# Norm statistics in a two-layer diffusion backbone: four channel chunks' matmuls issued side by side, squares of x kept in y

## The chip, the cores and the metric

One NeuronCore of a Trainium2 chip runs the whole forward pass. The metric is the time of one execution in microseconds of device time; of several runs the median is taken. Lower is better.

## What is computed

The reference is a backbone of two layers over 256 latent tokens and 256 context tokens, 1024 channels, all in float32. Every sub-layer (half feed-forward, mixer, half feed-forward) is wrapped in two RMS norms over the channels, one ahead of it and one behind it:

```
def rms_norm(x, gain):
    xf = x.astype(f32)
    xf = xf * lax.rsqrt(jnp.mean(jnp.square(xf), axis=-1, keepdims=True) + RMS_EPS)
    return (xf * gain.astype(f32)).astype(x.dtype)
def half_ffn(h, g_in, g_out, mod, w1, w3, w2):
    y = swiglu(pre_norm(h, g_in, mod), w1, w3, w2)
    return post_residual(h, y, g_out, mod, 0.5)
```

The mixer of layer 0 is a bidirectional S5 scan, that of layer 1 a differential attention. The change concerns only the mean of squares inside `rms_norm`.

## The kernel before, in words

Activations lie with channels on the 128 partitions: `x` and `y` are tiles [128, 2, 8, 256], that is two halves h (C = 0 the context, L = 1 the latents), eight channel chunks k, 256 tokens. The sum of squares over channels is therefore a sum over partitions and over k, and it is TensorE that forms it. `stat_add` (L213) does one chunk: ScalarE squares [128, 256] into a buffer `sq` (L216), and TensorE multiplies it by 32 columns of ones (L218) into 32 rows of a PSUM bank `st`, rows 32j with j = k mod 4, where chunks k and k + 4 add up. The buffers `sq` come from a pool of four (L53) that every user takes in the order of the program.

`stat_end` (L241) copies the bank (L245, VectorE), sums the four row groups by a small matmul (L248), takes the inverse root by Newton steps on two-element tiles (L225 to L234, VectorE), and spreads it over the partitions by another matmul (L255). There are 21 such statistics of eight chunks: 168 calls of `stat_add`.
- Ten stand behind a sub-layer. In the last pass of a feed-forward's second product (`ff2`, L487 and L488) output chunk d takes 12 or 18 matmuls of 256 columns (L372 to L374; float32 is split into a high and a low part, three products), VectorE adds them to y (L487), and `stat_add` follows for this d. The pass is done for half C, then for half L. The gate of S5 (`glu`, L1016) and the attention's output product (L1267) do the same.
- Eleven stand ahead of a sub-layer (`pre_stat`, L304): eight chunks of x, just after `post` (L277) has updated them on VectorE (L301). `pre` (L310) then writes y = x * scale * bc (L326) and its split into `hb` (L332, L333), on which the next products wait.

At a boundary of two sub-layers the program has this order: last pass for C, then post and pre for C, then last pass for L, then post and pre for L; the next sub-layer's first products begin with half C of its first three weight blocks. So C's norms run beside L's pass, and L's norms beside the next sub-layer's first products for C. Some matmuls are held back by hand: `QA = (0, 1, 6, 7)` lets the first products' chunk k = 0 follow L248 of L's post, k = 1 its L255, k = 6 the L248 of L's pre, k = 7 its L255 (`after` adds an order between two instructions of one engine).

The order on each engine is otherwise worked out ahead of the run by a planner that simulates the program; earlier instructions of the program have priority. The engines then run their lists strictly in order. Weights come by DMA into `stg`, ScalarE copies them to a high part `wh` (L352), VectorE forms the low part `wl` (L354). In layer 0's S5 part y is held in another layout ("mixed"): the chunks are interleaved in runs of 32 tokens, so that y[:, k] is a view of 8 runs; `yv(h, mixed)` (L261) gives either view.

One other place writes 32-row groups of one bank: `mod_pe` (L150) issues eight matmuls of 256 columns directly one after the other, over the four row groups twice.

Of the kernel before, what the change touches and what calls it, by code (L numbers as in the profile page):

```python
# [8 lines left out]
F32 = mybir.dt.float32  # L9
F32R = mybir.dt.float32r  # L10
I32 = mybir.dt.int32
AF = mybir.ActivationFunctionType
# [6 lines left out]
H = 256  # L19
# [13 lines left out]
class Net:  # L33
# [174 lines left out]


    def stat_begin(self):  # L210
        return self.ps_st.tile([128, 2 * H], F32, name="st")

    def stat_add(self, part, k, src):  # L213
        nc = self.nc
        sq = self.sq_p.tile([128, H], F32, name="sq")
        nc.scalar.activation(out=sq if len(src.shape) == 2 else sq.rearrange("p (t c) -> p t c", t=8), in_=src, func=AF.Square)  # L216
        j = k % 4
        nc.tensor.matmul(part[32 * j:32 * j + 32, 0:H], self.ones[:, 0:32], sq, start=(k < 4), stop=(k >= 4))  # L218

    def newton(self, r, v, n):  # L220

# [79 lines left out]
                    nc.vector.scalar_tensor_tensor(out=xk, in0=y[:, k], scalar=self.mod[:, l, s, 2, k, h:h + 1], in1=xk,  # L301
                                                   op0=ALU.mult, op1=ALU.add)

    def pre_stat(self, h):  # L304
        part = self.stat_begin()
        for k in range(ND):
            self.stat_add(part, k, self.x[:, h, k])
        return self.stat_end(part)

    def pre(self, l, s, h, split=True, mixed=False, bc=None, pool=()):  # L310
        nc = self.nc
        if bc is None:
            bc = self.pre_stat(h)
        if pool:
            bp = self.spread(bc)
        y = self.yv(h, mixed)
        los = []
        for k in range(ND):
            scale, shift = (self.mod[:, l, s, i, k, h:h + 1] for i in (1, 0))
            if k in pool:  # L320
                yk, xk = y[:, k], self.x[:, h, k].rearrange("p (t c) -> p t c", t=8)
                nc.gpsimd.tensor_tensor(out=yk, in0=xk, in1=bp.rearrange("p (t c) -> p t c", t=8), op=ALU.mult)
                nc.gpsimd.tensor_scalar(out=yk, in0=yk, scalar1=scale, scalar2=shift, op0=ALU.mult, op1=ALU.add)
                continue
            with self.after(los[k - 2] if split and k >= 2 else None):
                nc.vector.scalar_tensor_tensor(out=y[:, k], in0=self.x[:, h, k].rearrange("p (t c) -> p t c", t=8),  # L326
                                               scalar=scale, in1=bc.rearrange("p (t c) -> p t c", t=8),
                                               op0=ALU.mult, op1=ALU.mult)
            if split:
                hi, lo = (self.hh(h, j)[:, k] for j in range(2))  # L330
                yk = self.y[:, h, k]
                nc.scalar.activation(out=hi, in_=yk, func=AF.Identity, bias=shift)  # L332
                los.append(nc.vector.scalar_tensor_tensor(out=lo, in0=yk, scalar=shift, in1=hi,  # L333
                                                          op0=ALU.add, op1=ALU.subtract))
            else:
                nc.scalar.activation(out=y[:, k], in_=y[:, k], func=AF.Identity, bias=shift)
# [941 lines left out]
def body(tc, a, out, stop=None):  # L1278
    with ExitStack() as es:
        n = Net(tc, a, es)  # L1280
        nc = tc.nc
        L, C = 1, 0

        def dump():
            nc.sync.dma_start(out[1], n.x[:, 1])
            nc.scalar.dma_start(out[0], n.x[:, 0])

        def mods(*spec):
            def job(l, s, k, d):
                return 2.3, lambda: n.mod_job(l, s, k, d, n.last.ins)  # L1290
            return [job(l, s, k, d) for l, lst in zip(spec[::2], spec[1::2]) for s, k in lst for d in range(ND)]

        def steps(g, n, w):
            return [(w, lambda: next(g, None)) for _ in range(n)]

        def mix(*lists):

            order = sorted(((i + 0.5) / len(l), k, i) for k, l in enumerate(lists) for i in range(len(l)))
            return [lists[k][i] for _, k, i in order]

        def jobs0(es):
            i, o = n.s5_in_maps(), n.s5_out_maps()
            m = n.mod_pe([(0, 2), (1, 0), (1, 1), (1, 2), (2, 0), (2, 1)])
            return [(0.0, lambda: n.s5_maps_pool(es))] + mix(steps(i, 33, 3.0), steps(o, 42, 3.0), steps(m, 49, 1.5))

        for h, part in n.ffn(0, 0, (C, L), jobs0):
            if h == C:
                n.mod_fin(0, 0, (2,))
                n.mod_fin(0, 1, (0, 1, 2))
                n.mod_fin(0, 2, (0, 1))  # L1310
            n.post(0, 0, h, part, pool=(5, 6, 7) if h == L else ())
            if stop == "00":
                continue
            n.pre(0, 1, h, split=False, mixed=True, pool=(5, 6, 7) if h == L else ())
            if h == C:
                p0 = tc.cur_priority
        if stop == "00":
            return dump()

        def dumpm():  # L1320
            for h in range(2):
                nc.vector.tensor_copy(n.x[:, h].rearrange("p k (t c) -> p k t c", t=8), n.yv(h, True))
            dump()

        if stop == "h0":
            return dumpm()
        for h, part in n.s5(p0):
            if stop == "ymix0":
                continue
            n.post(0, 1, h, part, mixed=True)  # L1330
            if stop == "01":
                continue
            n.pre(0, 2, h)
        if stop == "ymix0":
            return dumpm()
        if stop == "01":
            return dump()
        for h, part in n.ffn(0, 2, (C, L), lambda es: mods(0, [(2, 2)], 1, [(0, 0), (0, 1), (0, 2), (1, 0), (1, 1)])):
            if h == C:
                n.mod_fin(0, 2, (2,))  # L1340
                n.mod_fin(1, 0, (0, 1))
            n.post(0, 2, h, part)
            if stop != "02":
                n.pre(1, 0, h)
        if stop == "02":
            return dump()
        for h, part in n.ffn(1, 0, (C, L), lambda es: mods(1, [(1, 2), (2, 0), (2, 1), (2, 2)])):
            if h == C:
                n.mod_fin(1, 0, (2,))
                n.mod_fin(1, 1, (0, 1))  # L1350
            n.post(1, 0, h, part)
            if stop != "10":
                n.pre(1, 1, h)
        if stop == "10":
            return dump()
        n.mod_fin(1, 1, (2,), (L,))
        n.mod_fin(1, 2, (0, 1, 2), (L,))
        part = n.attn()
        if stop == "ymix1":
            n.x = n.y  # L1360
            nc.vector.memset(n.y[:, 0], 0.0)
            return dump()
        n.post(1, 1, L, part, half=(4, 6))
        if stop == "11":
            return dump()
        n.pre(1, 2, L)
        for h, part in n.ffn(1, 2, (L,)):
            n.post(1, 2, h, part, half=(4, 6))
        if stop == "12":
            return dump()  # L1370
        for i, e in ((0, 2), (2, 4), (4, 6), (6, 8)):
            nc.sync.dma_start(out[0][:, i:e], n.x[:, 1, i:e])
# [88 lines left out]
```

## Time and profile before

| what | value |
|---|---|
| median of 3 runs | 1941.02 us (1938.6 to 1942.37) |
| profiled execution, its own time | 1940.48 us |
| its span in the trace | 1938.7 us |
| TensorE busy | 1807.7 us, 93% of the span |
| VectorE, ScalarE, GpSimd busy | 65%, 37%, 8% |
| L218, the statistics' matmuls: busy | 76.4 us, 336 instructions |
| L216, the squares: busy | 33.1 us from x, 30.7 us from y |

The span is the traced part of the execution; 1.8 us of the execution's time lie around it. A float32 matmul shows as two MATMUL instructions, so 168 calls are 336 rows. Matmuls overlap in the trace (the next begins while the last drains), so what a matmul costs the stream is read from start to start and not from its duration.

### The profile page before, as it was taken

How to read it: one execution, taken by the hardware profiler on the slowest of the kernel's cores; microseconds unless marked ns; L12 is line 12 of the kernel's file. 1: busy time of each engine (PE TensorE's matmuls, PEld its weight loads, DVE VectorE, ACT ScalarE, POOL GpSimd, SP SyncE). 2: the span in 40 equal slices, each digit the busy share in tenths (PEclk: the TensorE clock that was granted, in tenths of full speed). 3: DMA queues.
4: the chain of work that ended last, by engine and by line, in shares of the span. 5: the costliest groups of instructions: out<-in, count | busy, mean ns of one | idle time of the engine just before them, and what ended most of it. 6: DMA issues, size and time to landing. Idle time of an engine off the chain costs nothing.

```text
span 1938.7 us, 29411 instructions
## 1 busy us (share of the span) xinstructions
PE 1807.7 (93%) x11600; PEld 1503.7 (78%) x11600; DVE 1253.0 (65%) x2914; ACT 715.0 (37%) x1286; POOL 149.3 (8%) x250
## 2 busy tenths in 40 slices
PE   7999999999747889999999999999998999779997
PEld 3877777777637768888888798888887988669996
DVE  5868877642797567977763675455437587655554
ACT  4542332321534544222222343222224455544442
POOL 0123423320211000000000000000000000000000
PEclk8999999999968999999999999999999999989998
DMA  8678878882277634655543144444322221125551
GB/s 319 189 256 267 255 246 248 255 276 101 84 250 242 225 131 153 227 183 186 174 164 109 66 142 166 149 162 154 127 78 74 87 88 66 38 96 184 183 176 64
DMA packets 74954, 321.94 MB, mean 166 GB/s; under 512 B 13984, under 2 KB 15392, under 8 KB 54336
## 3 DMA queue, kind: packets, MB, share of 16 engines
q1 hardware_dynamic: 55472, 273.61, 40.7%
q0 software_dynamic: 19200, 45.40, 8.1%
q8 instruction: 91, 1.49, 0.3%
q10 hardware_dynamic: 144, 1.05, 0.1%
q14 instruction: 47, 0.39, 0.1%
HBM read 296.53 MB, written 23.53 MB: 165 GB/s over the span
## 4 chain that ended last, share of the span: by engine, by line
PE 81%; DVE 8%; DMA 6%; ACT 3%; issue 2%; POOL 1%; DVEq 0%; SPq 0%; ACTq 0%; POOLq 0%
PE mm L372 15%; PE mm L373 15%; PE mm L374 15%; PE acc L372 8%; PE acc L373 7%; PE acc L374 7%; PE st L218 3%; DMA bs<-bw 2%; DMA pt<-pqt 1%; DVE wl L354 1%; DMA ws<-cs 1%; PE acc L130 1%; PE st L255 1%; PE st L150 1%; PE mm L911 1%
## 5 line engine op out<-in xcount | busy, mean ns | idle before, releaser
L372 PE MATMUL mm<-hb,wh 128*128 128x512 f32 (+1 forms) x1632 | 573.8, 353 | 7.0 <-ACT wh L352 2.7
L373 PE MATMUL mm<-hb,wl 128*128 128x512 f32 (+1 forms) x1632 | 567.8, 350 | 0.0
L374 PE MATMUL mm<-hb,wh 128*128 128x512 f32 (+1 forms) x1632 | 560.1, 349 | 0.0
L352 ACT ACTIVATE wh<-stg 128x1024 fp32r<-128x1024 f32 x312 | 330.9, 1067 | 549.6 <-PE acc L374 302.3
L354 DVE TENSOR_TENSOR wl<-stg,wh 128x1024 fp32r<-128x1024 f32 x312 | 380.4, 1223 | 187.3 <-ACT wh L352 186.0
L372 PEld LDWEIGHTS mm<-hb,wh 128*128 128x128 f32 x1632 | 311.6, 191 | 60.7 <-issue 14.2
L373 PEld LDWEIGHTS mm<-hb,wl 128*128 128x128 f32 x1632 | 311.3, 191 | 44.1 <-issue 3.7
L374 PEld LDWEIGHTS mm<-hb,wh 128*128 128x128 f32 x1632 | 306.5, 191 | 43.0 <-issue 3.9
L372 PE MATMUL acc<-gh,wh 128*128 128x256 f32 (+1 forms) x832 | 282.8, 340 | 6.3 <-DVE y L496 4.7
L373 PE MATMUL acc<-gh,wl 128*128 128x256 f32 (+1 forms) x832 | 278.3, 335 | 0.0
L374 PE MATMUL acc<-gl,wh 128*128 128x256 f32 (+1 forms) x832 | 277.8, 335 | 0.0
L372 PEld LDWEIGHTS acc<-gh,wh 128*128 128x128 f32 x832 | 156.7, 188 | 33.2 <-DVE y L496 6.4
L373 PEld LDWEIGHTS acc<-gh,wl 128*128 128x128 f32 x832 | 156.7, 188 | 21.8 <-issue 5.1
L192 DVE CUSTOM_DVE_ANT_0 wjk<-wad,sb 128x1024 bf16<-128x1024 f32 x136 | 166.1, 1221 | 9.8 <-DMA wad<-wadat 7.9
L374 PEld LDWEIGHTS acc<-gl,wh 128*128 128x128 f32 x832 | 156.2, 188 | 19.2 <-issue 1.6
L496 DVE TENSOR_TENSOR y<-y,acc 128x512 f32<-128x512 f32 (+1 forms) x112 | 68.0, 608 | 89.4 <-PE acc L374 89.0
L445 DVE TENSOR_TENSOR si<-si,mm 128x512 f32<-128x512 f32 (+1 forms) x85 | 52.3, 616 | 97.8 <-PE mm L374 97.6
L443 ACT ACTIVATE si<-mm 128x512 f32<-128x512 f32 (+1 forms) x85 | 46.0, 541 | 166.6 <-PE mm L374 166.3
L218 PE MATMUL st<-sq,cst 128*32 128x256 f32 x336 | 76.4, 419 | 18.5 <-ACT sq L216 11.5
L487 DVE TENSOR_TENSOR y<-y,acc 128x256 f32<-128x256 f32 x56 | 22.9, 418 | 71.3 <-PE acc L374 71.2
L1074 POOL DMA_DIRECT2D rope<-rope x1 | 0.6, 567 | 849.0 <-PE acc L374 849.0
L339 ACT ACTIVATE gh<-si 128x512 fp32r<-128x512 f32 (+1 forms) x88 | 49.8, 566 | 43.4 <-DVE si L445 43.3
(403 smaller groups left out, 2186.0 us busy)
## 6 DMA issues: line engine op xcount, KB each, us to landing
stg<-w SPq DMA_DIRECT2D x132, 1024.0 KB, 4.9
wad<-wadat SPq DMA_DIRECT2D x80, 512.0 KB, 3.7
wad<-wadq SPq DMA_DIRECT2D x48, 512.0 KB, 6.9
ws<-cs SPq DMA_DIRECT2D x27, 512.0 KB, 11.2
bt<-s5bt POOLq DMA_DIRECT2D x32, 256.0 KB, 5.8
pt<-pqt POOLq DMA_DIRECT2D x32, 256.0 KB, 7.4
cs<-cw POOLq DMA_DIRECT2D x32, 256.0 KB, 5.1
bs<-bw POOLq DMA_DIRECT2D x32, 256.0 KB, 6.8
```

The lines of the kernel that those rows point to most:

```text
L192: nc.vector.tensor_tensor_reduce(out=jk, in0=w, in1=self.sb[:, h, :], op0=ALU.mult, op1=ALU.add, scale=1.0, scalar=0.0, accum_out=self.mod ...
L218: nc.tensor.matmul(part[32 * j:32 * j + 32, 0:H], self.ones[:, 0:32], sq, start=(k < 4), stop=(k >= 4))
L339: self.nc.scalar.activation(out=hi, in_=src, func=AF.Copy)
L352: nc.scalar.activation(out=hi, in_=st[:, o:o + w], func=AF.Copy)
L354: e.tensor_tensor(out=lo, in0=st[:, o:o + w], in1=hi, op=ALU.subtract)
L372: nc.tensor.matmul(out, wh, xh, start=first, stop=False)
L373: nc.tensor.matmul(out, wl, xh, start=False, stop=False)
L374: self.pe_last = nc.tensor.matmul(out, wh, xl, start=False, stop=last)
L443: nc.scalar.activation(out=si, in_=z1, func=AF.Silu)
L445: nc.vector.tensor_tensor(out=gf, in0=si, in1=z3, op=ALU.mult)
L487: nc.vector.tensor_tensor(out=yd, in0=yd, in1=o, op=ALU.add)
L496: nc.vector.tensor_tensor(out=yd, in0=yd, in1=o, op=ALU.add)
```

## The change

`stat_add` only collects the square; with every fourth chunk it issues the four matmuls in the order 3, 0, 1, 2, each ordered behind the last by `after`. For x the squares go into y[:, k] (in the layout y was last used in, `was=True` behind S5), for y into the four `sq` buffers as before. Nothing is added to the DMA queues.

```diff
     def stat_begin(self):
+        self.sqs = []
         return self.ps_st.tile([128, 2 * H], F32, name="st")
-    def stat_add(self, part, k, src):
-        nc = self.nc
-        sq = self.sq_p.tile([128, H], F32, name="sq")
-        nc.scalar.activation(out=sq if len(src.shape) == 2 else sq.rearrange("p (t c) -> p t c", t=8), in_=src, func=AF.Square)
-        j = k % 4
-        nc.tensor.matmul(part[32 * j:32 * j + 32, 0:H], self.ones[:, 0:32], sq, start=(k < 4), stop=(k >= 4))
+    def stat_add(self, part, k, src, sq=None):
+        nc = self.nc
+        if sq is None:
+            sq = self.sq_p.tile([128, H], F32, name="sq")
+        o = sq if len(src.shape) == len(sq.shape) else sq.rearrange("p (t c) -> p t c", t=8)
+        nc.scalar.activation(out=o, in_=src, func=AF.Square)
+        self.sqs.append(sq)
+        if k % 4 == 3:
+            last = None
+            for j in (3, 0, 1, 2):
+                po = part[32 * j:32 * j + 32, 0:H]
+                if len(self.sqs[j].shape) == 3:
+                    po = po.rearrange("p (t c) -> p t c", t=8)
+                with self.after(last):
+                    last = nc.tensor.matmul(po, self.ones[:, 0:32], self.sqs[j], start=(k < 4), stop=(k >= 4))
+            self.sqs = []
...
-    def pre_stat(self, h):
+    def pre_stat(self, h, mixed=False):
         part = self.stat_begin()
+        y = self.yv(h, mixed)
         for k in range(ND):
-            self.stat_add(part, k, self.x[:, h, k])
+            self.stat_add(part, k, self.x[:, h, k].rearrange("p (t c) -> p t c", t=8), y[:, k])
         return self.stat_end(part)
-    def pre(self, l, s, h, split=True, mixed=False, bc=None, pool=()):
+    def pre(self, l, s, h, split=True, mixed=False, bc=None, pool=(), was=False):
         nc = self.nc
         if bc is None:
-            bc = self.pre_stat(h)
+            bc = self.pre_stat(h, was)
...
             n.post(0, 1, h, part, mixed=True)
...
-            n.pre(0, 2, h)
+            n.pre(0, 2, h, was=True)
```

## Rows read from the trace of the kernel before

**Rows 1.** The profile's page: TensorE's busy time, and the chain that ended last by line (share of the span).
```profile
PE 1807.7 (93%) x11600; PEld 1503.7 (78%) x11600; DVE 1253.0 (65%) x2914; ACT 715.0 (37%) x1286; POOL 149.3 (8%) x250
PE mm L372 15%; PE mm L373 15%; PE mm L374 15%; PE acc L372 8%; PE acc L373 7%; PE acc L374 7%; PE st L218 3%; DMA bs<-bw 2%; DMA pt<-pqt 1%; DVE wl L354 1%; DMA ws<-cs 1%; PE acc L130 1%; PE st L255 1%; PE st L150 1%; PE mm L911 1%
```

**Rows 2.** The instructions of line 218 (duration in ns: least, median, longest), and the group of the squares of x in the list of groups (busy us, mean ns | idle before, and what ended it).
```profile
L218 PEld LDWEIGHTS st<-sq,cst x336: 106/109/155, 6.9 to 1923.8; 128*32 128x32 f32 x168
L218 PE MATMUL st<-sq,cst x336: 378/403/637, 6.9 to 1924.0; 128*32 128x256 f32 x168
L216 ACT ACTIVATE sq<-x 128x256 f32<-128x256 f32 x88 | 33.1, 413 | 35.3 <-DVE x L301 23.4 <-PE st L218 11.7
```

**Rows 3.** Timeline of TensorE in the last pass of a feed-forward (start us, length us): one call of `stat_add`, two records merged in one row, between the product's matmuls.
```profile
1052.26 0.28 PE L373 MATMUL acc<-gh,wl 128*128 128x256 f32 x1
1052.38 0.28 PE L374 MATMUL acc<-gl,wh 128*128 128x256 f32 x1
1052.58 0.62 PE L218 MATMUL st<-sq,cst 128*32 128x256 f32 x2
1053.13 0.39 PE L372 MATMUL acc<-gh,wh 128*128 128x256 f32 x1
1053.36 0.28 PE L373 MATMUL acc<-gh,wl 128*128 128x256 f32 x1
```

**Rows 4.** Timelines of TensorE and of its weight loads at one group of `mod_pe`: eight calls, 16 records merged in one row.
```profile
99.90 1.07 PE L150 MATMUL st<-wad,sk 128*32 128x256 f32 x16
99.89 0.59 PEld L150 LDWEIGHTS st<-wad,sk 128*32 128x32 f32 x16 [0.36 <-issue]
```

**Rows 5.** Timeline of TensorE: two calls of `stat_add` that came to stand together, and four that did, each with the matmul behind it.
```profile
1494.13 0.63 PE L218 MATMUL st<-sq,cst 128*32 128x256 f32 x4
1494.68 0.39 PE L1102 MATMUL sc<-wh,hb 128*128 128x256 f32 x1
...
1086.98 0.64 PE L218 MATMUL st<-sq,cst 128*32 128x256 f32 x8
1087.55 0.61 PE L248 MATMUL st<-cst,sb__10078 128*128 128x1 f32 x4
```

**Rows 6.** Line 218 alone by stretches (start:end, us; then length, TensorE busy with this line and records, weight loads busy and records; then for the stretch the granted clock as a share of 2.4 GHz, the DMA engines' busy share, GB/s).
```profile
468.00:484.00 16.00, 4.95 (x16) 1.10 (x16) 1.00 0.01 3
490.00:504.00 14.00, 4.20 (x32) 1.14 (x32) 0.97 0.52 192
630.00:647.00 17.00, 4.90 (x16) 1.22 (x16) 1.00 1.01 393
661.00:674.00 13.00, 2.50 (x16) 0.57 (x16) 0.90 0.35 129
681.00:698.00 17.00, 4.34 (x16) 0.97 (x16) 0.99 0.55 198
711.00:722.00 11.00, 4.95 (x16) 1.10 (x16) 1.00 0.00 1
1048.00:1068.00 20.00, 4.95 (x16) 1.10 (x16) 1.00 0.00 1
1079.00:1092.00 13.00, 4.67 (x32) 1.41 (x32) 1.00 0.34 112
1104.00:1114.00 10.00, 4.95 (x16) 1.10 (x16) 1.00 0.00 0
1440.00:1460.00 20.00, 4.95 (x16) 1.10 (x16) 1.00 0.00 1
1471.00:1484.00 13.00, 4.67 (x32) 1.41 (x32) 1.00 0.33 112
1493.00:1502.00 9.00, 3.73 (x16) 0.84 (x16) 1.00 0.01 2
1693.00:1710.00 17.00, 4.95 (x16) 1.10 (x16) 1.00 0.55 186
1716.00:1722.00 6.00, 4.93 (x16) 1.45 (x16) 0.52 0.00 0
1912.00:1925.00 13.00, 4.34 (x16) 0.97 (x16) 1.00 0.00 1
```

**Rows 7.** Timelines of ScalarE and VectorE beside the first products after the boundary at 1094 us: the squares of L's x, and the copy in `stat_end`.
```profile
1102.17 1.60 ACT L216 ACTIVATE sq<-x 128x256 f32<-128x256 f32 x4 [0.94 <-DVE x L301]
1105.22 0.42 ACT L216 ACTIVATE sq<-x 128x256 f32<-128x256 f32 x1 [1.44 <-PE st L218]
...
1113.52 0.43 DVE L245 COPY sb__10370<-st 128x256 f32<-128x256 f32 x1 [8.27 <-PE st L218]
```

**Rows 8.** Timelines of ScalarE and TensorE at the end of L's pass and the start of the next sub-layer, same boundary.
```profile
1087.09 1.06 ACT L352 ACTIVATE wh<-stg 128x1024 fp32r<-128x1024 f32 x1 [1.80 <-PE acc L374]
1088.05 1.32 ACT L216 ACTIVATE sq<-y 128x256 f32<-128x256 f32 x4
...
1088.50 1.54 PE L218 MATMUL st<-sq,cst 128*32 128x256 f32 x8 [0.35 <-ACT sq L216]
...
1094.05 0.58 PE L372 MATMUL mm<-hb,wh 128*128 128x256 f32 x1 [1.26 <-ACT hb L332]
```

**Rows 9.** Timelines of ScalarE and VectorE in S5's gate, where y is in the interleaved layout: chunks 0 to 3 are written by L998, chunks 4 to 7 by L949.
```profile
654.78 1.33 ACT L998 ACTIVATE y<-y 128x256 f32<-128x256 f32 x4
...
662.36 0.87 DVE L949 TENSOR_TENSOR y<-y,mm 128x128 f32<-128x128 f32 x4
```

## The prediction on record

> **What bounds the kernel now.** I read the page first: TensorE is busy for 93% of the span, and the chain that ended last is nearly all TensorE, the statistics' line with 3% of it, some 60 us [rows 1]. Next the line itself. Each of its 336 records is a matmul of at least 378 ns with a weight load of 109 ns [rows 2]. Last the timeline around one call, since durations overlap. The product's matmuls follow at 0.12 us from start to start. With one call between them, 0.98 us pass from the matmul ahead of it to the second one behind it, where two steps of 0.12 would do [rows 3]. So **one call costs the stream 0.74 us**: 0.20 before the call starts, 0.55 to the next matmul, and that one's step is 0.23. A stretch table of this line shows where the calls stand: 4.95 us busy for 16 records is eight times the 0.62 us of one call, hence eight separate islands, at a granted clock of 1.00 and with hardly any DMA [rows 6].
>
> **What a group of four costs.** The rows already hold groups. Two calls side by side take 0.55 us to the next matmul, the same as one, and four take 0.57 us [rows 5]. In the group of eight calls over the four row groups, 16 matmuls end within 1.07 us and their 16 loads within 0.59 us [rows 4]. Run in turn at the 0.24 us by which the second record of a lone call follows the first (0.62 us for both, less the 0.38 us of one [rows 2, 3]), the 16 would take over 3.8 us. I take 0.76 us for a group in the stream. Four lone calls cost 2.96, so a full group gives back **2.20 us**.
>
> At this place a rule of the Trainium skill speaks against the change. In "TensorE: Matmul & The Clock Gate", part 3, "What overlaps and what doesn't", it says that a weight load overlaps matmuls in flight only when its row group differs; these four share all rows and differ in columns. By that rule a group would cost about 2.8 us and the change would give almost nothing; the trace disagrees with it [rows 4, 5].
>
> **The sum, stage by stage** (records and busy time from rows 6; busy time over 0.62 is the number of islands).
> - C's last pass in three feed-forwards (468, 1048, 1440 us): eight islands each, six full groups, 13.2 us. The stream behind it is L's pass on the same engine, so the time passes through.
> - Norms of L's x beside the next first products (711, 1104 us): eight islands each, four groups, 8.8 us. At 1493 us there are six islands: 6 x 0.74 - 2 x 0.76 = 2.9. It would not count if L's norm then came too late. Today the fifth square waits 1.44 us for a `sq` buffer, that is for a matmul, and the copy behind the last matmul starts at 1113.52 although the fourth square was done at 1103.8 [rows 7]. With squares in y this wait is gone: eight squares of 0.41 us [rows 2] could be done by 1106, some 6 us ahead of today's copy. The held-back products k = 6 and 7 stay covered.
> - S5's second half, 661 and 681 us: four islands become two, 1.4 us; seven become one in the stream and one at its end, where I leave out two that already stand at the tail: 5 x 0.74 - 0.76 = 2.9.
> - Output product of the attention and the very last pass (1693, 1912 us): the second group ends the pass with nothing behind it. I count the first group whole and half the second: 3.3 each, 6.6.
> - Three tails (490, 1079, 1471 us), where C's norm of x and L's norm of y meet: 4.2 to 4.7 us of TensorE busy time become four groups of about 0.6, so 1.8 to 2.2 less. L's squares need `sq` buffers that C's earlier squares hold today; four of them come in a row after the last matmul and a weight copy of 1.06 us, and their matmuls take until 1090.04 [rows 8]. After, only the last should be left there. I take 2.0 each, 6.0. The bounds are 0 (a VectorE chain sets the end anyway) and 3.
> - S5's gate for C (630 us): up to 3.3 us of islands, but the DMA engines are busy throughout, 1.01 at 393 GB/s, with the scan's maps that the next products need [rows 6]. I take 0.5; bounds 0 and 3.3.
> - The start, the norm at 504 us (already grouped) and the one at 1716 us: nothing. At 1716 the clock is at 0.52, that is 1.2 GHz, for VectorE and ScalarE set the pace [rows 6]; a group is no later than its last square.
>
> What is added: nothing on DMA, POOL or SP. The number and shape of the squares stay. Squares written to y come from the same instruction that releases x, so no new wait on VectorE. In the interleaved layout the views of two chunks interlock; a tracking by whole ranges would hold every square of S5's norm until the last read of y. It does not seem to be so: chunks 0 to 3 are rewritten by ScalarE 7 us before VectorE adds to chunks 4 to 7 [rows 9]. The price would be some 3 us in two places where the stream covers it. A group does wait for its fourth square, while the first three lie done; on TensorE everything planned behind it waits too. Cover for that is the plan: the next chunk's 12 to 18 matmuls, 1.4 to 2.1 us, can go ahead, against 0.42 us of addition and 0.41 of square.
>
> Sum: 13.2 + 8.8 + 2.9 + 1.4 + 2.9 + 6.6 + 6.0 + 0.5 = **42.3 us**. The profiled execution took 1940.48 us (span 1938.7 and 1.8 around it), 0.5 below the median of the three runs. 1941.0 - 42.3 gives **1898.5 us**, 2.2% faster.
>
> **The rivals.**
> 1. *The boundaries take it back.* The stream gets shorter, but the next sub-layer starts when C's Newton steps and `hb` are done, as at 1094 us, where TensorE waits 1.26 us for `hb` [rows 8]. If the stretches beside the norms give nothing (8.8 + 2.9), the tails nothing (6.0) and S5 only half of 4.3, 20 us remain lost: about 1919. For it: the steps on VectorE are a serial chain, off TensorE. Against: C's chain also begins earlier by what C's pass saves.
> 2. *Not side by side.* If the order 3, 0, 1, 2 makes each matmul wait for the one before, three further calls cost 2 x 0.24 us each: a group is 0.74 + 1.44 = 2.18, gives back 0.78 instead of 2.20, and the total is 42.3 x 0.78 / 2.20 = 15 us, 1926. With the loads in turn as well (8 x 0.109 us in all [rows 2], 0.22 more per call) a group is 2.84 and the total 2.3 us: 1939, no change. The rule cited above would give this second case. Against both: the groups of rows 4 and 5.
> 3. *Slower: groups stall TensorE.* TensorE takes its list in order. If the plan puts a group right behind its simulated fourth square and the real square is late, behind weight copies of 1.06 us on ScalarE [rows 8], all matmuls wait. 42 groups make up for 42.3 us when each stalls 1.0 us on average; at one copy and one square each, 1.06 + 0.41, the loss is 62 us and the time about 1960. For it: copies do stand before squares at the tails. Against: with one call per chunk the same risk exists today, and the stretches at 1048 and 1440 us run at full clock with calls a whole chunk apart.
> 4. *The plan gets better than I count.* Tails at 3 us each, the gate at 3.3, the L half's first products half a microsecond earlier in three places: 7 us more, 1891.
>
> **How the numbers follow.** Forecast (with small deviations of its terms) 0.68; rival 1 0.12; rival 2 0.05, of which 0.02 for no change; rival 3 0.05; rival 4 0.10. The range 1887 to 1921 holds the forecast, rival 4 and rival 1 with their spread: the unknown terms are the tails (0 to 9), the gate (0 to 3.3) and the last pass. What is left out is rivals 2 and 3 and misses on either end. A measurement of this kernel can tell about 0.2%, 3.9 us, from no change: faster 0.92, same 0.03, slower 0.05.
>
> **What would show it.** In the changed trace L218 stands in rows of x8, 0.64 us long, 0.57 us from start to the next matmul; its busy time falls from 76.4 to about 28 us (42 x 0.64, more where the clock is low). C's pass at 1048 us is 4.4 us shorter. L216 from x no longer waits for L218. L218's idle time before it stays small. It is wrong if the four records' starts lie 0.24 us apart or more, if TensorE idles ahead of L218 in the stream, or if the stretch from the last matmul of L's pass to the next first product grows by what the passes save.

## The result, and the profile after

The changed kernel takes **1890.01 us** (median of 4 runs, 1886.6 to 1893.54) against 1939.81 for the kernel before (4 runs, 1930.89 to 1942.37): ratio **0.9743**, 95% interval 0.9709 to 0.9777. A second comparison on another chip gave 0.9785 (0.9755 to 0.9816; 1897.89 against 1937.57 us). The change is worth 2.2 to 2.6%; the forecast, 1898.5 of 1941.0, is a ratio of 0.978.

The page of the changed kernel, beside [rows 1]: TensorE has the same 11600 instructions and 49.6 us less busy time, and the statistics' line (now L229) has 1% of the chain where it had 3%.
```profile
PE 1758.1 (93%) x11600; PEld 1494.9 (79%) x11600; DVE 1253.9 (66%) x2914; ACT 716.4 (38%) x1286; POOL 149.5 (8%) x250
PE mm L386 16%; PE mm L387 16%; PE mm L388 16%; PE acc L386 8%; PE acc L388 8%; PE acc L387 8%; DVE wl L368 1%; DMA bs<-bw 1%; PE st L150 1%; PE st L229 1%; DMA ws<-cs 1%; ACT wh L366 1%; PE st L762 1%; PE mm L925 1%; DMA zl<-ts 1%
```

One group in the stream, C's last pass (timeline of TensorE: start us, length us), beside [rows 3].
```profile
1028.15 0.28 PE L387 MATMUL acc<-gh,wl 128*128 128x256 f32 x1
1028.36 0.64 PE L229 MATMUL st<-sq,cst 128*32 128x256 f32 x8
1028.93 0.39 PE L388 MATMUL acc<-gl,wh 128*128 128x256 f32 x1
1029.15 0.28 PE L386 MATMUL acc<-gh,wh 128*128 128x256 f32 x1
```
Eight records in one row: from the matmul ahead (1028.15) to the second behind (1029.15) 1.00 us pass, where two steps of 0.12 would do. A group costs the stream 0.76 us, as forecast, and one call had cost 0.74. Inside the row (the same timeline for 1028.37 to 1028.59 us and for 1028.80 to 1028.92) four records start together and the other four 0.24 us later:
```profile
1028.36 0.42 PE L229 MATMUL st<-sq,cst 128*32 128x256 f32 x4
1028.60 0.40 PE L229 MATMUL st<-sq,cst 128*32 128x256 f32 x4
```
One record lasts 0.40 or 0.38 us [rows 2], and four of them fill 0.42 and 0.40: they begin within 0.02 us of each other. So the four calls run side by side, first their first records, then their second ones.

Line 229 by stretches (columns as in [rows 6]), with the whole span last: 29.64 us busy for the same 336 records, where L218 had 76.4.
```profile
455.00:471.00 16.00, 1.28 (x16) 0.31 (x16) 1.00 0.22 82
471.00:487.00 16.00, 2.35 (x32) 0.73 (x32) 0.96 0.68 241
619.00:636.00 17.00, 1.28 (x16) 0.32 (x16) 1.00 1.03 407
1028.00:1039.00 11.00, 1.28 (x16) 0.31 (x16) 1.00 0.00 0
1051.00:1060.00 9.00, 2.35 (x32) 0.73 (x32) 0.96 0.43 131
1075.00:1080.00 5.00, 1.28 (x16) 0.31 (x16) 1.00 0.01 3
1673.00:1678.00 5.00, 2.16 (x16) 0.43 (x16) 0.50 0.00 0
0.00:1890.60 1890.60, 29.64 (x336) 7.32 (x336) 0.96 0.50 170
```
1.28 us for 16 records is two groups of 0.64: the eight islands of [rows 6] became two, in C's passes (455, 1028 us), at S5's gate (619) and beside L's first products (1075).

ScalarE and VectorE beside the first products after the boundary at 1062 us, in answer to [rows 7].
```profile
1071.36 3.25 ACT L220 ACTIVATE y<-x 128x256 f32<-128x256 f32 x8 [3.07 <-DVE x L313]
...
1078.51 0.43 DVE L257 COPY sb__10306<-st 128x256 f32<-128x256 f32 x1 [4.42 <-PE st L229]
```
Eight squares run in one piece into y and wait for no matmul.

**Where the time went.** The programs were profiled again, and the table goes by marks that both have on TensorE: first products of a sub-layer, the small matmul of a named norm. Stretches are in us; the before column has two executions, the after column three, in the order profiled.

| stretch | before | after | mean gain | forecast |
|---|---|---|---|---|
| start to the first `mod_pe` call | 99.9, 100.8 | 97.4, 96.7, 101.7 | 1.8 | 0 |
| first to last `mod_pe` call | 345.0, 338.1 | 338.0, 343.6, 339.5 | 1.2 | 0 |
| C's last pass, first feed-forward | 39.2, 39.2 | 34.7, 34.7, 34.7 | 4.5 | 4.4 |
| the two feed-forwards up to C's norm at 1062 and 1440 us (the pass is in it) | 346.0 each | 341.3, 341.3, 341.4 and 341.6, 341.3, 341.6 | 4.7, 4.5 | 4.4 each |
| tail into S5, and S5 to the norm of its gate for C | 163.8, 163.6 | 160.6, 159.5, 156.2 | 4.9 | 2.5 |
| from there to the second feed-forward's first product | 51.8, 51.3 | 46.3, 47.3, 47.1 | 4.7 | 4.3 |
| beside first products (to L's norm of x), three places | 60.3, 64.2 | 52.7, 53.4, 53.7 | 9.0 | 11.7 |
| tails at 1062 and 1440 us | 52.6, 52.3 | 50.7, 50.3, 50.4 | 2.0 | 4.0 |
| attention to L's norm of its output | 205.2, 206.8 | 201.0, 199.9, 198.9 | 6.1 | 3.3 |
| tail into the last feed-forward | 17.3, 17.9 | 17.7, 18.1, 17.7 | -0.2 | 0 |
| last feed-forward to L's norm, with the very last pass | 197.9, 197.9 | 195.0, 195.0, 195.0 | 2.9 | 3.3 |
| end | 13.8, 13.8 | 13.5, 13.5, 13.5 | 0.3 | 0 |

The mean spans differ by 46 us (1938.3 and 1892.3). The first two rows, 3.0 of it, vary by more than that between executions of one program (below). Without them 43 us remain, against the 42.3 forecast, with terms that miss on either side (see the part on the prediction).

### The profile page after: what moved, and what is told of

The parts are those of the page before. It is cut to its first block, busy times and chain, and to the rows that moved or that the text cites. A ratio compares the mean times of both kernels' runs of the same rounds, so it can differ in the third digit from the quotient of the medians.

```text
span 1890.6 us, 29388 instructions
## 1 busy us (share of the span) xinstructions
PE 1758.1 (93%) x11600; PEld 1494.9 (79%) x11600; DVE 1253.9 (66%) x2914; ACT 716.4 (38%) x1286; POOL 149.5 (8%) x250
## 4 chain that ended last, share of the span: by engine, by line
PE 83%; DVE 7%; ACT 4%; DMA 4%; issue 1%; POOL 0%; DVEq 0%; ACTq 0%; SPq 0%; POOLq 0%
PE mm L386 16%; PE mm L387 16%; PE mm L388 16%; PE acc L386 8%; PE acc L388 8%; PE acc L387 8%; DVE wl L368 1%; DMA bs<-bw 1%; PE st L150 1%; PE st L229 1%; DMA ws<-cs 1%; ACT wh L366 1%; PE st L762 1%; PE mm L925 1%; DMA zl<-ts 1%
## 5 line engine op out<-in xcount | busy, mean ns | idle before, releaser
L368 DVE TENSOR_TENSOR wl<-stg,wh 128x1024 fp32r<-128x1024 f32 x312 | 380.5, 1224 | 187.1 <-ACT wh L366 186.4
L387 PEld LDWEIGHTS acc<-gh,wl 128*128 128x128 f32 x832 | 156.2, 188 | 16.8 <-issue 0.2
L346 ACT ACTIVATE hb<-y,mod 128x256 fp32r<-128x256 f32 x72 | 35.2, 506 | 64.2 <-DVE y L340 63.4
L501 DVE TENSOR_TENSOR y<-y,acc 128x256 f32<-128x256 f32 x56 | 22.9, 419 | 51.3 <-PE acc L388 51.2
```

The costliest lines, as they stand in the source:

```text
L368: e.tensor_tensor(out=lo, in0=st[:, o:o + w], in1=hi, op=ALU.subtract)
L387: nc.tensor.matmul(out, wl, xh, start=False, stop=False)
L501: nc.vector.tensor_tensor(out=yd, in0=yd, in1=o, op=ALU.add)
```

## The experiments

The theory: a matmul of 32 columns in the stream of 128-column tiles costs about as much alone as in a group of four, so time falls by the number of islands. The rivals: the squares kept in y are what helps; any grouping, without side by side work, is enough; or the gain lies elsewhere.

### Fours kept, squares of x back in `sq`
```
-  self.stat_add(part, k, self.x[:, h, k].rearrange("p (t c) -> p t c", t=8), y[:, k])
+  self.stat_add(part, k, self.x[:, h, k])
```


> As the change, but the squares of x go into the four sq buffers as before. Theory A (what pays is the time that four matmuls side by side take off TensorE's stream; y only keeps the buffers from holding up ScalarE): most of the gain stays, some 5 us are lost at the three tails and in the stretches beside the next first products, about 1896 against 1890. Rival B (without y the groups of C's x and L's y must take the four buffers in turn, and every boundary waits): 15 us or more lost, 1905 or later, with ScalarE's squares waiting for the statistics' matmuls by more than the 11.7 us of before.

Measured: 1917.76 us (1912.29 to 1922.62) against 1938.49; ratio 0.989 (0.987 to 0.991). About half of the gain is gone: 1.1% is left of 2.2 to 2.6%. So the expectation that the buffers hardly matter fell. By the marks of the table this kernel loses 8.8 us in S5 up to its gate, 8.0 beside the first products and 2.7 in the two tails, against the means of the changed one. The waits point to the buffers (us in all, times, longest), of this kernel, of the changed one and of the kernel before:
```profile
ACT sq L220 <- PE st L229: 33.9, 19, 5.8
```
```profile
ACT sq L220 <- PE st L229: 14.1, 7, 3.1
```
```profile
ACT sq L216 <- PE st L218: 13.4, 17, 1.6
```
Four squares now hold all four buffers until their group has run. The timelines of ScalarE and TensorE, and the windows after the boundary (length, TensorE, weight loads, VectorE, ScalarE, GpSimd busy, granted clock, DMA share, GB/s), show what that does:
```profile
1087.02 1.60 ACT L220 ACTIVATE sq<-x 128x256 f32<-128x256 f32 x4 [4.47 <-DVE x L313]
1091.76 1.34 ACT L220 ACTIVATE sq<-x 128x256 f32<-128x256 f32 x4 [3.13 <-PE st L229]
```
```profile
1082.80 1.22 PE L267 MATMUL st<-cst,nr 128*128 128x128 f32 x4 [2.23 <-DVE nr L246]
```
```profile
1080.00:1084.00 4.00, 1.77 (x8) 1.47 (x8) 3.14 (x14) 1.52 (x3) 0.00 (x0) 0.50 0.00 0
1084.00:1088.00 4.00, 4.00 (x21) 4.00 (x20) 3.94 (x8) 0.98 (x3) 0.00 (x0) 0.50 0.00 0
1088.00:1092.00 4.00, 4.00 (x33) 3.46 (x32) 1.70 (x5) 0.87 (x3) 0.00 (x0) 0.87 0.00 0
```
L's norm is late (TensorE idles 2.23 us for it), TensorE restarts at a granted clock of 0.50, that is 1.2 GHz, and the second four squares wait 3.13 us for the first group. The stretch beside these first products is 22.0 us, where the changed kernel's three executions had 16.5 to 17.7 and the kernel before 20.8 and 20.9.

### Squares of x in y, no fours
```
-  if k % 4 == 3: ... for j in (3, 0, 1, 2): ...
+  j = k % 4
+  nc.tensor.matmul(po, self.ones[:, 0:32], sq, start=(k < 4), stop=(k >= 4))
```


> The squares of x go into y, but each square has its own matmul as soon as it is done, as before. Theory A: the 0.74 us islands stay, so C's passes at 1048 and 1440 us keep their length; only the tails (2 us each), the start and the wait for sq go: about 1930 against 1940. Rival B (the buffers were what held the boundaries): a third or more of the gain, 1923 or earlier.

Measured: 1935.5 us (1926.82 to 1940.69) against 1938.49; ratio 0.9978 (0.996 to 0.9996). C's pass takes 39.2 us as before. The buffers alone give about 3 us, at the edge of what can be told, and not the 10 expected: the two tails that the table names, which were to give 2 us each, take 52.3 us, as before. Yet no square waits for the statistics' matmuls any more (13.4 us in 17 waits before), so these waits cost little as long as the calls are single.

### Fours for y only, x one by one in `sq`
```
-  if k % 4 == 3:
+  if not four or k % 4 == 3:
...
+  self.stat_add(part, k, self.x[:, h, k], four=False)
```


> Only the statistics behind the sub-layers (squares of y) are issued in fours; those ahead of them are as before, in sq and one by one. Theory A, by the terms of the prediction: C's passes 13.2, output products 6.6, S5's gate 3.4 and a part of the tails stay, some 24 us: about 1916. The stretches beside the next first products (711, 1104, 1493 us) keep their six to eight islands. Rival B (the gain hangs on y holding the squares of x): under 12 us, 1928 or later.

Measured: 1918.0 us (1911.04 to 1928.55) against 1938.49; ratio 0.9887 (0.986 to 0.9915), as expected. Line 229 beside L's first products, the columns of [rows 6]: eight islands, as before.
```profile
1094.00:1106.00 12.00, 4.95 (x16) 1.10 (x16) 1.00 0.00 0
```
Side by side: nothing 1938.5, y as the place alone 1935.5, fours for y alone 1918.0, fours for all without y as the place 1917.8. Fours for x on top of fours for y gain nothing (0.2 us) while the four `sq` buffers are shared; with the squares in y they gain the rest, 21 to 29 us by the two ratios of the changed kernel. Neither half does it alone.

### The four calls into the same rows
```
-  po = part[32 * j:32 * j + 32, 0:H]
+  po = part[0:32, 0:H]
```
All eight chunks add up in rows 0 to 31; the copy and the small matmul then use 32 rows.

> As the change, but the four matmuls of a group all go into the same 32 rows of the bank (the copy and the small matmul behind it then use these 32 rows alone), so they cannot run side by side. Theory A: a group in the stream costs 0.74 + 3 x 0.48 = 2.18 us instead of 0.76; with some 19.5 groups in the stream 28 us come back: about 1918. Rival C (grouping alone pays, by fewer changes between 128 and 32 columns): 1892, as the change.

Measured: 1946.26 us (1942.32 to 1958.06) against 1938.49; ratio 1.0035 (1.0014 to 1.0056). It was to be faster than before, by less; it is slower. TensorE, one group in C's pass:
```profile
1058.75 0.28 PE L387 MATMUL acc<-gh,wl 128*128 128x256 f32 x1
1058.96 1.91 PE L229 MATMUL st<-sq,cst 128*32 128x256 f32 x8
1060.80 0.38 PE L388 MATMUL acc<-gl,wh 128*128 128x256 f32 x1
```
The group takes 1.84 us to the next matmul, not 0.57. In C's passes that still saves 2.0 us (37.1, 344.1 and 344.0 us). What the expectation left out are the groups at tails, which before already stood side by side [rows 5] and now run in turn: tail into S5 (to its L925, before L911) 33.7 us, tails at 1062 and 1440 us 27.2 and 30.0, into the last feed-forward 20.4, where before had at most 29.8, 25.2, 27.5 and 17.9; the table's two S5 rows are longer too, 173.5 and 55.3 us against 163.8 and 51.8. Over 42 groups, 1.84 less 0.57 is 53 us; the two comparisons of the changed kernel lie 0.025 to 0.029 below this ratio, 48 to 57 us. So **without the side by side work nothing of the gain is left**. In the stream the group in turn still costs 2.03 us (worked as in [rows 3]) where four lone calls cost 2.96: of a group's 2.20 us, 0.93 come from three interruptions fewer and 1.27 from working side by side. What the stream saves so is lost again at the tails and in S5.

In "TensorE: Matmul & The Clock Gate", part 3, the Trainium skill lets a weight load overlap matmuls in flight only when its row group differs. Here not even the group that shares rows and columns follows that. TensorE and its loads, for 1059.41 to 1059.42 us:
```profile
1059.20 0.59 PE L229 MATMUL st<-sq,cst 128*32 128x256 f32 x2
1059.41 0.11 PEld L229 LDWEIGHTS st<-sq,cst 128*32 128x32 f32 x1
```
Two matmuls of 0.38 us fill 0.59, so the second starts at 1059.41. The load starts with it and is done after 0.11 us, ahead of the matmul that follows 0.21 us later. So a load goes while a matmul in its own rows has just begun, and a further call costs two such steps, 0.42 us.

### The order 0, 1, 2, 3 without the tie
```
-  for j in (3, 0, 1, 2):
+  for j in range(4):
...
-  with self.after(last):
+  with self.after(None):
```


> As the change, but the four matmuls in the order 0, 1, 2, 3 and with no order set between them. Theory A: the planner places each as its square comes, so a part of the groups falls apart into single calls and up to half of the gain goes, 1900 to 1912. Rival F (ordering is of no account, the planner keeps them together by priority): 1890 as the change, L229 in rows of x8.

Measured: 1926.7 us (1922.4 to 1931.24) against 1942.27; ratio 0.9921 (0.9897 to 0.9946). Worse than expected: about two thirds of the gain are lost. TensorE, C's first pass:
```profile
463.59 0.62 PE L229 MATMUL st<-sq,cst 128*32 128x256 f32 x2
...
465.87 0.62 PE L229 MATMUL st<-sq,cst 128*32 128x256 f32 x2
...
468.04 0.62 PE L229 MATMUL st<-sq,cst 128*32 128x256 f32 x2
```
Free of the tie the planner issues a call as soon as its square is there, and single calls stand in the stream again. In the change the call j = 3 at the head needs the last square, and the others are tied behind it, so they come together. This run takes away the order and the tie at once; what either does alone was not tried.

### A pool of its own for the squares of x, in place of y
```
+  n.sq2 = n.pool("sq2", 4)
...
+  self.stat_add(part, k, self.x[:, h, k], self.sq2.tile([128, H], F32, name="sqx"))
```
The pool serves the last seven norms of x, from the one for C ahead of the second feed-forward on (56 squares); the four ahead of it, both of S5's among them, put their 32 squares in y as in the change. The expectation says S5's second norm; it starts one sub-layer later.

> As the change, but from S5's second norm on the squares of x go into four buffers of their own, not into y (for the earlier norms there is no room, they stay in y). Theory G (what y saves is that C's x and L's y take the same four buffers in turn): as the change, 1889 to 1895. Rival H (x needs room for all eight squares, since with four the second group's squares wait for the first group's matmuls, which the plan puts a whole chunk later): half of what squares in sq lose comes back at most, 1899 to 1908, and ScalarE waits for L229 beside the next first products.

Measured: 1898.39 us (1892.86 to 1915.39), the changed kernel beside it 1897.89 (1893.23 to 1901.01; expected as follows), before 1937.57.

> The changed kernel in five rounds, as a measure for the other two of this call: 0.974 of the kernel before, 1890 to 1893.

The ratios are 0.981 (0.9771 to 0.9849) and 0.9785 (0.9755 to 0.9816): no difference that the spread can tell. So for these seven norms it is not y as the place that matters, nor room for all eight squares of x; it is enough that squares of x and of y no longer take turns at the same four buffers. Whether a common pool of eight would do as well was not tried. Squares of x do wait for their own pool (here at L230):
```profile
ACT sqx L221 <- PE st L230: 10.9, 6, 4.5
```
yet the stretches beside the first products stay short (20.9, 16.3, 17.1 us; the changed kernel 20.4 to 21.9, 16.5 to 17.7, 14.9 to 15.8).

### Both programs once more, and the change at the start only
The first profiles differ by 7.0 us in the stretch of `mod_pe` (L150), which the change doesn't touch. Three runs ask whether that belongs to the change: the two programs again, and one in which only the two norms at the start have fours and squares in y.

> The kernel before, once more, for a second profile. Theory D (the 7 us that the stretch from the first to the last group of mod_pe, 99.9 to 444.9 us, is shorter after the change come from another order of the plan and repeat): 345 us again, within 2. Rival E (they are a matter of the execution, since DMA queues pace this stretch): the length moves by 4 us or more between two executions of the same program.

> The changed kernel, once more. Theory D: the same stretch takes 338 us again, within 2. Rival E: it moves by 4 us or more. The passes of half C (346.0 to 341.5 us from norm to norm) repeat within 0.3 either way.

> The change only in the two norms ahead of the first sub-layer; all others as before. Theory D: the start is 2 to 3 us shorter (first group of mod_pe at 97.4 as in the changed kernel) and the new plan carries into the stretch behind it: about 1931 against 1939. Rival E: the start alone, 1936 to 1939.

Measured: 1939.72, 1896.55 and 1939.19 us (1932.47 to 1948.29), the last against 1942.27: ratio 0.9987 (0.9969 to 1.0004). Line 150 (duration least, median, longest; first and last start), in turn before, before again, after, after again:
```profile
L150 PE MATMUL st<-wad,sk x384: 379/379/403, 99.9 to 445.6; 128*32 128x256 f32 x192
```
```profile
L150 PE MATMUL st<-wad,sk x384: 379/379/403, 100.8 to 439.6; 128*32 128x256 f32 x192
```
```profile
L150 PE MATMUL st<-wad,sk x384: 379/379/404, 97.4 to 436.1; 128*32 128x256 f32 x192
```
```profile
L150 PE MATMUL st<-wad,sk x384: 379/379/404, 96.7 to 441.1; 128*32 128x256 f32 x192
```
From first to last 346, 339, 339 and 344 us: either program has the short and the long form. The stretch varies by execution, and the change at the start gains nothing that can be told.

### TensorE kept busy across the boundary
The first products after a boundary start at a granted clock of 0.50 to 0.66 in both kernels (mean of their first 2 us). Five useless matmuls of 128x240 between `stat_end`'s small matmul and its last one, at five norms, were to keep it up.
```
+  for _ in range(warm):
+      with self.after(cm_ins):
+          nc.tensor.matmul(part[:, H + 8:H + 248], self.eye, self.cst[:, 0:240], start=True, stop=True)
```


> As the change, plus five matmuls of no use (128 x 240, 0.4 us each) between the small matmul and the Newton steps of the last norms of five boundaries (L's norm behind a sub-layer in three feed-forwards and the attention, and the norm of x behind the attention), where TensorE stands idle and the first products then run at a granted clock of 0.50 for 3 to 4 us. Theory W (the clock falls for want of work there, and 1.5 to 2 us go at each): 1882 to 1886. Rival I (the clock falls all the same, or the filler is itself in the way of C's chain): 1890 to 1898.

Measured: 1908.79 us (1899.02 to 1918.2); ratio 0.984 (0.9807 to 0.9873), so some 11 us slower than the change beside it. TensorE at the boundary at 1075 us:
```profile
1068.77 4.35 PE L264 MATMUL st<-cst 128*128 128x240 f32 x10
1072.91 1.06 PE L271 MATMUL st<-cst,nr 128*128 128x128 f32 x4
1075.09 0.58 PE L390 MATMUL mm<-hb,wh 128*128 128x256 f32 x1 [1.12 <-ACT hb L350]
```
The filler takes 4.35 us and C's last small matmul stands behind it in TensorE's list, so the first product is later: that tail is 27.6 us against 23.7 to 23.9, and the one into the last feed-forward 23.1 against 17.7 to 18.1. Nor did it keep the clock up there: the ten records ran at 0.50 themselves, and the first 2 us of the products behind them too. The same holds at 1694 and 1703 us, ahead of the last feed-forward. Only at the attention's first product (1462.7 us) was the clock at 1.00, and the stretch beside it still took 16.4 us, against 14.9 to 15.8 without the filler. So both parts of rival I are seen; a gain from the clock is not, and a filler that costs no time was not tried.

## Why the prediction was right, step by step

- **The price of a group** was read from groups that the rows held by chance, and held exactly: 0.76 us in the stream, 0.64 us a row, 29.64 us busy against "about 28". The two cases of rival 2 (2.18 and 2.84 us a group) are out; the kernel with the same rows shows what the first of them looks like: 2.03 us, worked as in [rows 3].
- **C's passes**: 13.2 forecast, 13.7 measured, the same within 0.3 us in every execution. The sum's largest term is also its surest: what the islands give back here, the pass gets shorter by.
- **Beside the first products**: 11.7 forecast, 9.0 measured. The reason given was that squares in y free ScalarE from waiting for matmuls. Borne out is that x's squares need buffers apart from y's: without them fours for x are worth 0.2 us. That every wait must go is not: in the pool of its own they wait 10.9 us, and the three stretches are as short. The size varies (18.3 and 16.3 us before in the attention, 14.9 to 15.8 after), since TensorE's clock is low there for a time that differs by execution (below).
- **Tails**: this step failed in size. 2.0 each was taken, 1.4 and 0.6 measured at 1062 and 1440 us, and 1.0 at the tail into S5 (to its first product, L856, now L870: 21.6 and 21.8 us, then 20.5 to 21.0). Groups of 0.64 us and a single one at the end came as forecast, but the lower bound's reason, that VectorE sets the end, mostly decides. TensorE at 1440 us shows it, beside [rows 8]:
```profile
1439.72 0.64 PE L229 MATMUL st<-sq,cst 128*32 128x256 f32 x8 [1.11 <-ACT sq L220]
1442.90 1.01 PE L260 MATMUL st<-cst,sb__13175 128*128 128x1 f32 x4 [2.54 <-DVE sb__13175 L257]
1445.22 2.33 PE L267 MATMUL st<-cst,nr 128*128 128x128 f32 x8 [1.31 <-DVE nr L246]
1447.55 0.79 PE L1116 MATMUL mm<-wh,hb 128*128 128x256 f32 x2
```
  Between the last group and the first product TensorE idles 2.54 and 1.31 us for VectorE. VectorE is not idle there: the copy that the first wait is for (L257, 1442.43 us) comes behind small pieces of the attention (L1106, L1107) and the low part of a weight (L368, 1.23 us). That the last square still comes behind a weight copy was foreseen too (ScalarE, at 1062 us):
```profile
1056.30 1.06 ACT L366 ACTIVATE wh<-stg 128x1024 fp32r<-128x1024 f32 x1 [2.12 <-PE acc L388]
1057.27 0.40 ACT L220 ACTIVATE sq<-y 128x256 f32<-128x256 f32 x1
```
- **Attention's output**: 3.3 forecast, 6.1 measured. The step counted the second group half, since it ends the pass. But its first three calls stood in the stream, and only the last stood at the end, where the group now stands at the same price: it counts whole, 4.4. In the very last pass only one call of the second half stood in the stream (two came together at 1922.77 us, the last at 1923.80): 2.20 + 0.74 = 2.94, and 2.9 was measured for the forecast 3.3. The attention's other 1.7 us lie within the spread of executions: 198.9 to 201.0 after, and before 205.2, 206.8 and, in the kernel with the change at the start only, 203.9. Within that spread the kernel with the same rows (204.3) decides nothing.
- **S5 up to its gate for C**: 2.5 forecast (a tail of 2.0 and 0.5 at the gate), 4.9 measured, of which the tail is 1.0. The other 3.9 lie inside S5, from its first product to the norm of its gate: 142.2 and 141.7 us before, 139.6, 139.1 and 135.6 after, a spread of 4 us in one kernel. What the gate's groups give was not the reason: fours for y alone, which have them, take 164.8 us in the table's stretch, no less than before. The kernels with fours for x and y and x's squares of S5 in y are short (156.2 to 160.6; 158.4 with the later pool); those with one of the two are not (167.6 and 166.4). Which wait inside S5 goes was not found. The second half, 4.7 against 4.3, came as worked out.
- **The sum**: 43 us against 42.3 is closer than its terms are. The three tails (3.0 of 6.0) and the stretches beside the first products (9.0 of 11.7) gave 5.7 us less than forecast; S5 inside (3.9 for 0.5) and the attention's output (6.1 for 3.3) gave 6.2 more. That the two cancel is luck. The price of a group and the passes are not.
- **Rivals**: boundaries took back some 6 us (tails and the stretches beside the first products, 5.7 below the forecast) and not 20. From the last matmul of L's pass to the next first product the time did not grow by what the passes save: 7.0 us before and 6.2 to 6.4 after at 1062 us, 8.9 to 9.2 and 9.2 to 9.3 at 1440. Groups do wait more for squares, but not in the stream: TensorE's idle time before the line's matmuls rises from 18.5 to 24.2 us in all, and what is over 1 us of it stands at the start (7.76), at the end of passes (1.11, 1.11, 1.72 and, in S5, 3.25) and where squares set the pace anyway (5.23 at 1673 us, where two waits before had 3.0). In C's pass at 1028 us and beside L's first products at 1075 there is none. The better plan (1891) was the time of the first comparison, not its mechanism: the tails gave less than forecast, and the surplus of that profile came from its `mod_pe` stretch (7.0) and from S5.

## What to carry to other kernels

Where a narrow matmul is scattered through a stream of full tiles, its cost here was the interruption, not the columns (0.74 us for one, 0.76 for four): collect as many as there are column groups and tie them so that the last to be ready goes first. Before grouping, count the buffers that a group holds: a pool that was enough for singles makes whole groups wait for each other, and here that took about half of the gain. Read the forecast's price from groups that the trace already has, and look for those that stand together already, which gain nothing from grouping.

## What the runs showed of the hardware

- Four float32 matmuls of 128x32 weights by 256 columns, into four row groups of a bank, take 0.57 us to the next matmul, the same as one (0.55); the same four into one row group take 1.84. Into four groups, the first records of all four start within 0.02 us.
- After a boundary the clock comes back after a time that one program does not repeat. TensorE from the first product of the attention on, changed kernel, windows of 2 us (columns as in the windows above):
```profile
1447.50:1449.50 2.00, 1.99 (x10) 1.95 (x10) 1.97 (x4) 0.91 (x2) 0.00 (x0) 0.50 0.00 0
1449.50:1451.50 2.00, 2.00 (x11) 2.00 (x11) 2.00 (x5) 0.00 (x0) 0.00 (x0) 0.50 0.00 0
1451.50:1453.50 2.00, 2.00 (x18) 2.00 (x17) 2.00 (x7) 1.60 (x4) 0.00 (x0) 0.92 0.00 0
```
  The same place had 0.50 and 0.78 before 1.00 in the changed kernel's second profile, 0.64 and 1.00 in its third. In the kernel before it was 0.63 and 1.00 once, and 0.50, 0.50, 0.60 and 1.00 the other time. In the rows shown a window holds 10 or 11 matmuls at 0.50 and 18 at 0.92. So a stretch behind a boundary differs by a few microseconds between executions, and one pair of profiles can't price a change there.
